# Low parts of split weights and rotary products moved from GpSimd to VectorE, and two buffers of the last layer moved to tiles that are no longer read

## The chip, the cores and the metric

The kernel runs on one core of a Trainium2 chip. The metric is the device time of one execution in microseconds (us), lower is better. The core has a matrix engine (TensorE, PE in the rows; its weight loads are PEld), VectorE (DVE), ScalarE (ACT), GpSimd (POOL) and a queue that issues transfers from device memory (SyncE, SP). Each engine takes its instructions in a fixed order; semaphores tie the engines together.

## The reference, cut to what matters

Two layers over 256 latent tokens and 256 context tokens, model width 1024. Each layer is a half-step SwiGLU, a token mixing, and a second half-step SwiGLU. In the last layer, the context tokens only give keys and values to the mixing, and the last SwiGLU runs for latent tokens alone.

```
f0/f1:  x = x + 0.5 * gate * rmsnorm((silu(y @ wg) * (y @ wu)) @ wd)      # y = modulated rmsnorm(x), wg/wu 1024 x 2816
mixing: uv, q, k, v = split(y @ w_in)
        q, k = rope(q), rope(k)              # x * cos + rotated(x) * sin, latent tokens only
        o = [gMLP gating, differential attention, windowed attention] @ w_out
        x = x + gate * rmsnorm(o)
```

## The kernel before

**Split products.** A matrix product in full precision is made of three cheaper ones. A weight tile is loaded as fp32 into a staging buffer (`stg`, three of them), ScalarE rounds it to `hi` (L233), and the low part `lo = full - hi` is a subtraction (`split_lo`, L101). TensorE then adds hi x hi, hi x lo and lo x hi. `split` (L215) cuts a tile in two or four pieces along its depth; each piece is one ScalarE instruction and one subtraction. The `hi` and `lo` buffers are three each (`wsp`), handed out in rotation; a fourth tile waits until TensorE has read the first for the last time. `wchunk` is a load followed by a split.

**Who subtracts.** With `share=True` the first piece of a tile goes to GpSimd, the others to VectorE. Shared are the weights of the token mixing (`cols`, `wv`, and `chunk` of the first layer's output projection) and the first gate and up tiles of every SwiGLU but the very first (`two` in `ffn`). The rotary embedding (`rope_evac`) is a copy by ScalarE (L690), then a shuffle (L692), a product with the sine (L693), a product with the cosine on GpSimd (L694) and a sum (L695), the other three on VectorE.

**The order.** The program is written in the order of TensorE's work; tasks (softmax chains, turns of the normalised rows) are put in at due times counted in TensorE columns, and the framework orders each engine's queue by readiness and priority. The residual chains and `first=True` splits have high priority.

**The end of the last mixing and the last SwiGLU.** `rest_tokens` (L1010) computes the last gMLP parts and the output projection for the two latent token blocks: `wr` holds two weight tiles (columns 0 to 511), `wc` two more (columns 512 to 1023, the second of them in the place of Yh and Yl that the context tokens had). The norm gate's two rows (`gate_rows`, L416) are loaded into `CU[:, 7]` and `VGf[:, 3584:4096]`, parts of tiles that the mixing uses for queries, keys and values, and are read when the projection is scaled (L1071). The tile `CU` has the tag `Ul`, `QK` the tag `Uh`: the last SwiGLU's `Uh` and `Ul` lie in the same memory and can be written when the mixing's last instruction on `QK` and on `CU` is done. The last SwiGLU begins with two groups for each token block: the first gate and up tile, then the second gate and up tile (256 columns each). The first gate, the first up and the second up tile take `wsp` buffers, behind `wr` and `wc[0]` in the rotation; the second gate tile is split into the upper halves of `Uh` and `Ul`.

Of the kernel before, what the change touches and what calls it, by code (L numbers as in the profile page):

```python
# [15 lines left out]
ALU = mybir.AluOpType  # L16
# [9 lines left out]
KB = D // P  # L26
# [37 lines left out]
def trunk(ctx: ExitStack, tc: tile.TileContext, x, c, cx, c_ctx, w_mod, b_mod, norm_pre, norm_post,  # L64
# [32 lines left out]
    def f32(ap):  # L97
        return ap.bitcast(F32)

    def split_lo(lo, full, hi, eng=nc.vector):  # L100
        eng.tensor_tensor(lo, full, f32(hi), op=ALU.subtract)  # L101


    evq, clk, busy = [], [0.0], [False]
# [107 lines left out]
                return split(v, *args[1:], **kw)  # L212
        return split(stage(*args), *args[1:], **kw)

    def split(v, nk, ncol, pair=False, into=None, share=False, pool=False):  # L215
        if into is not None:
            hi, lo = into
        else:
            hi = wsp.tile([P, 2048], F32R, tag="hi", name=nm("hi"))[:, 0:nk * ncol].rearrange(
                "p (k c) -> p k c", k=nk)  # L220
            lo = wsp.tile([P, 2048], F32R, tag="lo", name=nm("lo"))[:, 0:nk * ncol].rearrange(
                "p (k c) -> p k c", k=nk)
        if pair:
            v4 = v.rearrange("p k (v g d) -> p k v g d", v=2, g=2)
            for g in range(2):
                hv = hi[:, :, g * P:(g + 1) * P].rearrange("p k (v d) -> p k v d", v=2)
                lv = lo[:, :, g * P:(g + 1) * P].rearrange("p k (v d) -> p k v d", v=2)
                nc.scalar.activation(hv, v4[:, :, :, g, :], AF.Copy)
                split_lo(lv, v4[:, :, :, g, :], hv)
            return hi, lo  # L230
        cut = [0, nk // 4, nk // 2, nk // 2 + nk // 4, nk] if nk >= 8 else [0, nk // 2, nk]
        for a, b in zip(cut, cut[1:]):
            nc.scalar.activation(hi[:, a:b, :], v[:, a:b, :], AF.Copy)  # L233
            split_lo(lo[:, a:b, :], v[:, a:b, :], hi[:, a:b, :],
                     nc.gpsimd if pool or (share and a == 0) else nc.vector)
        return hi, lo

    def acc3(o, terms):
# [294 lines left out]
                task(("y", s), turn_y(ys, nxt, st, s[0], *((pb, T_LATE, 1.2) if s == order[-1] else (pa,))))  # L533


    def gate_up(l, e, cs, into=None, share=False):
        return (wchunk([(0, 256, w_gate[l, e, :, cs:cs + 256])], KB, 256, into=into, share=share),
                wchunk([(0, 256, w_up[l, e, :, cs:cs + 256])], KB, 256, share=share))

    def gate_up_one(l, e, cs):  # L540
        return wchunk([(0, P, w_gate[l, e, :, cs:cs + P]), (P, 256, w_up[l, e, :, cs:cs + P])], KB, 256)
# [1 line left out]
    def ffn(l, e, streams, nxt, first=None, out_order=None):  # L543
# [36 lines left out]
        for pi, (f0, nf) in enumerate(PHASES):  # L580
            Uh = big.tile([P, KB, NT], F32R, tag="Uh", name=nm("Uh"))
            Ul = big.tile([P, KB, NT], F32R, tag="Ul", name=nm("Ul"))
            for fp in range(0, nf, 2):
                cs = (f0 + fp) * P
                two = pi == 0 and fp == 0 and not first
                if pi == 0 and fp == 2 and not first:
                    continue
                rows = nxt is None
                if first and pi == 0 and fp == 0:
                    for i in range(3):  # L590
                        hidden(first[i], first[3 + i], i, full)
                    step()
                    continue
                if first and pi == 0 and fp == 2:
                    gu = [pa(), pa()]
                    w = gate_up_one(l, e, cs + P)
                    for i in range(2):
                        acc3(gu[i], yterms(w, i * P, full))
                    hidden(gu[0], gu[1], 3, full)
                    step()  # L600
                    continue
                wg, wu = gate_up(l, e, cs, share=two)
                if two:
                    into = [t[:, 4:8, :].rearrange("p a (b c) -> p (a b) c", b=2)
                            for t in (Uh, Ul)]
                    second = gate_up(l, e, cs + 256, into, True)
                    for s in range(2) if rows else streams:
                        drain(("y", s))
                        for f, (g_, u_) in ((0, (wg, wu)), (2, second)):
                            if rows:  # L610
                                gu = pa()
                                acc3_multi([(gu[:, c0:c0 + 256], rterms(w, s), c0 == 0)
                                            for w, c0 in ((g_, 0), (u_, 256))])
                                task("u", hidden_rows(gu, f, s))
                                continue
                            gus = [pa(), pa()]
                            groups = []
                            for w, c0 in ((g_, 0), (u_, 256)):
                                for i in range(2):
                                    groups.append((gus[i][:, c0:c0 + 256], yterms(w, i * P, s),  # L620
                                                   c0 == 0))
                            acc3_multi(groups)
                            for i in range(2):
                                hidden(gus[i][:, 0:256], gus[i][:, 256:512], f + i, s)
                else:
                    for i in range(2):
                        g = pa()
                        acc3(g[:, 0:n], yterms(wg, i * P, ys))
                        u = pa()
                        acc3(u[:, 0:n], yterms(wu, i * P, ys))  # L630
                        hidden(g[:, 0:n], u[:, 0:n], fp + i, full)
                step()

            drain("u")
            down(l, e, pi, f0, nf, Z, Uh, Ul, out_order or streams, nxt)
# [40 lines left out]
    def mixing(l, streams, qstreams, nxt):  # L676
# [12 lines left out]
        def rope_evac(dst, ps, scale):  # L689
            nc.scalar.activation(dst, ps, AF.Copy, scale=scale)  # L690
            sh = wk.tile([P, 256], F32, tag="t256", name=nm("shf"))
            nc.vector.stream_shuffle(sh, dst, shmask)  # L692
            nc.vector.tensor_tensor(sh, sh, ropet[:, 1, :], op=ALU.mult)  # L693
            nc.gpsimd.tensor_tensor(dst, dst, ropet[:, 0, :], op=ALU.mult)  # L694
            nc.vector.tensor_tensor(dst, dst, sh, op=ALU.add)  # L695

        def fm(w, f0, s):
# [10 lines left out]
                nc.scalar.activation(dst[:, SEQ:NT], ps[:, o:o + CTX], AF.Copy, scale=scale)  # L708

        def cols(c0, n, into=None):  # L710
            return wchunk([(0, n, W[:, c0:c0 + n])], KB, n, into=into, share=True, first=True)

        tmpw = big.tile([P, 2, KB, 256], F32R, tag="Ul", name=nm("tmpw"))
        wkq = []
# [21 lines left out]
        def rows_of(k0, n, c0, w):  # L736
            return W[k0 * P:(k0 + n) * P, c0:c0 + w]

        wv = [wchunk([(0, 512, rows_of(k0, n, VB0, 512)), (512, 640, rows_of(k0, n, VC0, P))], n, 640,
                     share=True, first=True)  # L740
              for k0, n in ((0, 3), (3, 3), (6, 2))]

        def tok_terms(ws, tb, c0, c1):
# [276 lines left out]
        def rest_tokens():  # L1020
# [19 lines left out]
            wu = cols(U0, 256)  # L1040
            for m in (("m", l, 1), ("m",) + nxt[:2]):
                drain(m)
            gp = gate_rows(l, 1, 0, [CU[:, 7, :], VGf[:, 3584:4096]])
            gate_values(wg, (0, 1))
            wr = [out_rows(kk) for kk in range(2)]
            gates(wu, XS)
# [67 lines left out]
            return (QK[:, 4 + 2 * i:6 + 2 * i, SEQ:NT] if i < 2 else CU[:, 2 * i - 3:2 * i - 1, SEQ:NT])  # L1114

        def chunk(hf, i):
            return wchunk([(0, 512, w_out[l, i * 512:(i + 1) * 512, hf * 512:(hf + 1) * 512])], 4, 512,
                          share=True)

        def oterms(ws, tb):  # L1120
            return [(Yh[:, k, ycols(tb)], Yl[:, k, ycols(tb)], ws[k // 4][0][:, k % 4, :],
# [195 lines left out]
```

## Time and profile before

| | |
|---|---|
| time, median of 3 runs | 1740.14 us (1739.44 to 1740.27) |
| the profiled execution: its time | 1744.91 us |
| its span, first to last instruction | 1743.1 us |
| TensorE busy in it | 1708.0 us (98%) |
| VectorE busy | 1257.9 us (72%) |
| GpSimd busy | 156.0 us (9%) |
| granted TensorE clock, mean | 0.995 |

The busy time of an engine is the union of its instructions' spans; a wait stands as idle time of the engine that waits, with the instruction that ended it. The granted clock is 1.00 at 2.4 GHz and 0.50 at 1.2 GHz. A row of several instructions begins with the start of the first.

### The profile page before, as it was taken

The numbers are of one execution on the slowest core, as the hardware profiler recorded it, in microseconds if no ns is written. First come the engines' busy times: TensorE is split into PE (matmuls) and PEld (weight loads), VectorE is DVE, ScalarE is ACT, GpSimd is POOL, SyncE is SP. The second block draws the span as 40 slices with busy tenths as digits, with TensorE's granted clock in tenths as the row PEclk, the third lists the DMA queues.
The fourth block names the chain that finished last, engine by engine and source line by source line (L and its number), as shares of the span: only waits on it lengthen the run. The fifth ranks groups of instructions, "written<-read, shape, count | busy, mean of one in ns | idle before, by whom it ended". The sixth has DMA issues, their size and how long they took to land.

```text
span 1743.1 us, 24539 instructions
## 1 busy us (share of the span) xinstructions
PE 1708.0 (98%) x9551; PEld 1448.2 (83%) x9551; DVE 1257.9 (72%) x2272; ACT 689.8 (40%) x1460; POOL 156.0 (9%) x161
## 2 busy tenths in 40 slices
PE   7999999999999999999999999999999999999998
PEld 4788888889977789888888898888888897789997
DVE  5889969965578577799694578799674747765555
ACT  4333213244376562332223442322232626655443
POOL 0000000022222120000000210000000322010000
PEclk9999999999999999999999999999999999999999
DMA  9666546523131143565453235655444223226552
GB/s 336 192 197 201 189 137 193 196 78 109 59 124 42 45 128 128 182 195 192 145 187 128 73 122 169 193 192 194 140 152 145 73 86 121 73 92 200 194 193 85
DMA packets 193264, 256.13 MB, mean 147 GB/s; under 512 B 7466, under 2 KB 128508, under 8 KB 193148
## 3 DMA queue, kind: packets, MB, share of 16 engines
q1 hardware_dynamic: 192380, 254.51, 44.9%
q8 instruction: 75, 1.23, 0.3%
q14 instruction: 41, 0.34, 0.1%
q0 software_dynamic: 768, 0.05, 0.0%
HBM read 253.44 MB, written 1.10 MB: 146 GB/s over the span
## 4 chain that ended last, share of the span: by engine, by line
PE 86%; DVE 7%; ACT 3%; issue 2%; POOL 1%; DMA 1%; POOLq 0%; DVEq 0%; ACTq 0%; SPq 0%
PE pa L243 27%; PE pa L247 13%; PE pb L262 6%; PE pb L256 6%; PE pb L264 6%; PE pa L256 5%; PE pa L264 5%; PE pa L262 5%; PE pb L243 3%; DVE lo L101 2%; PE pb L247 2%; PE pa L1242 1%; PE pa L785 1%; PE pc L806 1%; PE pc L883 1%
## 5 line engine op out<-in xcount | busy, mean ns | idle before, releaser
L101 DVE TENSOR_TENSOR lo<-stg,hi 128x512 fp32r<-128x512 f32 (+3 forms) x476 | 369.1, 808 | 154.4 <-ACT hi L233 127.7
L233 ACT ACTIVATE hi<-stg 128x512 fp32r<-128x512 f32 (+3 forms) x496 | 318.4, 702 | 356.1 <-PE pa L243 119.9
L243 PE MATMUL pa<-Yl,hi 128*128 128x512 f32 (+1 forms) x1168 | 415.5, 365 | 0.0
L243 PE MATMUL pa<-Yh,hi 128*128 128x512 f32 (+1 forms) x1168 | 413.2, 363 | 0.0
L349 DVE SCALAR_TENSOR_TENSOR acc<-stg,sT,acc 128x512 f32<-128x512 f32 x448 | 308.4, 746 | 9.3 <-DMA stg<-in_w_mod_dram 9.3
L247 PE MATMUL pa<-Yh,lo 128*128 128x512 f32 (+1 forms) x1168 | 258.7, 363 | 0.0
L243 PEld LDWEIGHTS pa<-Yl,hi 128*128 128x128 f32 x1168 | 220.5, 189 | 34.5
L243 PEld LDWEIGHTS pa<-Yh,hi 128*128 128x128 f32 x1168 | 220.5, 189 | 33.7
L247 PEld LDWEIGHTS pa<-Yh,lo 128*128 128x128 f32 x1168 | 202.0, 189 | 34.4 <-DVE lo L101 0.2
L256 PE MATMUL pb<-hi,Ul 128*128 128x512 f32 x400 | 156.9, 392 | 0.0
L264 PE MATMUL pb<-lo,Uh 128*128 128x512 f32 x400 | 155.8, 390 | 0.0
L262 PE MATMUL pb<-hi,Uh 128*128 128x512 f32 x400 | 155.6, 390 | 0.1
L558 ACT ACTIVATE Uh<-ha 128x512 fp32r<-128x512 f32 (+1 forms) x92 | 50.7, 551 | 220.6 <-DVE ha L556 220.6
L554 ACT ACTIVATE ht<-pa 128x512 f32<-128x512 f32 (+1 forms) x91 | 46.4, 510 | 131.9 <-PE pa L247 109.2
L262 PE MATMUL pa<-Yh,hi 128*128 128x256 f32 x368 | 91.9, 285 | 0.0
L264 PE MATMUL pa<-Yl,hi 128*128 128x256 f32 x368 | 91.3, 283 | 0.0
L556 DVE TENSOR_TENSOR ha<-ha,pa 128x512 f32<-128x512 f32 (+1 forms) x91 | 53.2, 584 | 49.0 <-PE pa L247 48.2
L262 PEld LDWEIGHTS pb<-hi,Uh 128*128 128x128 f32 x400 | 75.1, 188 | 16.0 <-DVE Z L491 0.5
L264 PEld LDWEIGHTS pb<-lo,Uh 128*128 128x128 f32 x400 | 75.1, 188 | 15.5
L256 PEld LDWEIGHTS pb<-hi,Ul 128*128 128x128 f32 x400 | 75.1, 188 | 15.4
L264 PEld LDWEIGHTS pa<-Yl,hi 128*128 128x128 f32 x368 | 70.6, 192 | 0.1
L262 PEld LDWEIGHTS pa<-Yh,hi 128*128 128x128 f32 x368 | 70.5, 192 | 0.1
(300 smaller groups left out, 2700.3 us busy)
## 6 DMA issues: line engine op xcount, KB each, us to landing
stg<-in_w_mod_dram SPq DMA_DIRECT2D x64, 1024.0 KB, 5.1
stg<-in_ffn_w_gate_dram SPq DMA_DIRECT2D x42, 1024.0 KB, 5.3
stg<-in_ffn_w_up_dram SPq DMA_DIRECT2D x42, 1024.0 KB, 5.4
stg<-in_ffn_w_down_dram SPq DMA_DIRECT2D x32, 1024.0 KB, 5.1
stg<-in_w_in_dram SPq DMA_DIRECT2D x14, 1024.0 KB, 5.0
stg<-in_ffn_w_down_dram SPq DMA_DIRECT2D x16, 768.0 KB, 4.4
mst<-in_w_mod_dram SPq DMA_DIRECT2D x16, 512.0 KB, 8.9
stg<-in_w_out_dram SPq DMA_DIRECT2D x8, 1024.0 KB, 6.8
```

Of the source, the lines that this page charges most:

```text
L101: eng.tensor_tensor(lo, full, f32(hi), op=ALU.subtract)
L233: nc.scalar.activation(hi[:, a:b, :], v[:, a:b, :], AF.Copy)
L243: nc.tensor.matmul(o, lhsT=ah, rhs=r, start=(i == 0), stop=(i == n - 1))
L247: nc.tensor.matmul(o, lhsT=al, rhs=bh, start=(i == 0), stop=(i == n - 1))
L256: nc.tensor.matmul(o, lhsT=al, rhs=bh, start=False, stop=last, skip_group_check=True)
L262: nc.tensor.matmul(o, lhsT=ah, rhs=bh, start=(first and k == 0), stop=False, skip_group_check=True)
L264: nc.tensor.matmul(o, lhsT=ah, rhs=bl, start=False, stop=False, skip_group_check=True)
L349: nc.vector.scalar_tensor_tensor(a, v[:, k, :], sc, a, op0=ALU.mult, op1=ALU.add)
L554: nc.scalar.activation(t, g, AF.Tanh, scale=0.5)
L556: nc.vector.tensor_tensor(a, a, u, op=ALU.mult)
L558: nc.scalar.activation(uh, a, AF.Copy)
L785: nc.tensor.matmul(sc[:, 0:n], lhsT=QK[64 * m:64 * m + 64, 4 + h, tb * P:(tb + 1) * P], rhs=QK[64 * m:64 * m + 64, h, k0:k1], start=True, ...
```

## The change

The argument that sent a piece to GpSimd is gone: every low part is a VectorE subtraction. The rotary product with the cosine is on VectorE too. In the last layer, the norm gate's rows go to `S[:, 2]`, the residual stream's rows of a context token block, which nothing reads after the first SwiGLU of that layer. In the last SwiGLU, the first gate tile takes the upper halves of `Uh` and `Ul` and the second gate tile takes a `wsp` buffer; in the other SwiGLUs the second gate tile stays in `Uh` and `Ul`.

```diff
-    def split_lo(lo, full, hi, eng=nc.vector):
-        eng.tensor_tensor(lo, full, f32(hi), op=ALU.subtract)
+    def split_lo(lo, full, hi):
+        nc.vector.tensor_tensor(lo, full, f32(hi), op=ALU.subtract)
...
             nc.scalar.activation(hi[:, a:b, :], v[:, a:b, :], AF.Copy)
-            split_lo(lo[:, a:b, :], v[:, a:b, :], hi[:, a:b, :],
-                     nc.gpsimd if pool or (share and a == 0) else nc.vector)
+            split_lo(lo[:, a:b, :], v[:, a:b, :], hi[:, a:b, :])
...
-                wg, wu = gate_up(l, e, cs, share=two)
+                into = [t[:, 4:8, :].rearrange("p a (b c) -> p (a b) c", b=2) for t in (Uh, Ul)]
+                wg, wu = gate_up(l, e, cs, into if two and rows else None)
                 if two:
-                    into = [t[:, 4:8, :].rearrange("p a (b c) -> p (a b) c", b=2)
-                            for t in (Uh, Ul)]
-                    second = gate_up(l, e, cs + 256, into, True)
+                    second = gate_up(l, e, cs + 256, None if rows else into)
...
-            nc.gpsimd.tensor_tensor(dst, dst, ropet[:, 0, :], op=ALU.mult)
+            nc.vector.tensor_tensor(dst, dst, ropet[:, 0, :], op=ALU.mult)
...
-            gp = gate_rows(l, 1, 0, [CU[:, 7, :], VGf[:, 3584:4096]])
+            gp = gate_rows(l, 1, 0, [S[:, 2, 0:512], S[:, 2, 512:1024]])
```

The other lines of the diff take `share=True` out of `gate_up`, `cols`, `wv` and `chunk`. `rows` is true in the last SwiGLU alone.

## Rows read from the trace of the kernel before

**Rows 1.** The page: the span, and the busy time of TensorE with its share.

```profile
span 1743.1 us, 24539 instructions
...
PE 1708.0 (98%) x9551; PEld 1448.2 (83%) x9551; DVE 1257.9 (72%) x2272; ACT 689.8 (40%) x1460; POOL 156.0 (9%) x161
```

**Rows 2.** The busy time by stretch, of all engines. Columns: the stretch, its length, then busy us and instructions of each engine, the mean granted clock, the DMA engines' busy share and their GB/s. The stretches are the start, the attention part of the first layer's mixing and of the second's, the first groups of the last SwiGLU, and the end.

```profile
0.00:30.00 30.00, 18.64 (x126) 11.90 (x127) 13.61 (x46) 13.48 (x25) 3.92 (x14) 1.00 1.00 333
...
480.00:600.00 120.00, 113.73 (x744) 89.37 (x742) 83.25 (x225) 80.12 (x240) 22.17 (x17) 0.97 0.20 67
...
1440.00:1540.00 100.00, 96.06 (x611) 75.66 (x610) 72.82 (x168) 70.80 (x188) 15.97 (x14) 0.98 0.25 85
1540.00:1560.00 20.00, 16.62 (x121) 15.79 (x119) 13.63 (x24) 8.15 (x21) 4.07 (x4) 0.91 0.61 197
...
1710.00:1743.10 33.10, 25.77 (x130) 21.66 (x128) 15.12 (x21) 9.50 (x16) 4.32 (x4) 0.95 0.13 48
```

**Rows 3.** Who TensorE waited for, in three stretches, one after the other: 480 to 660 us, 1380 to 1540 us, 1540 to 1560 us. Columns: waiting instruction, what ended the wait, us in total, times, longest us.

```profile
PE pa L769 <- DVE p L796: 2.9, 4, 1.5
...
PE pb L243 <- POOL lo L101: 0.5, 1, 0.5
...
PE pa L264 <- DVE lo L101: 2.0, 2, 1.5
PE pa L262 <- ACT hi L233: 0.7, 1, 0.7
PE pa L264 <- POOL lo L101: 0.6, 1, 0.6
```

**Rows 4.** GpSimd's subtractions (L101) and its rotary products (L694), in the views of these two lines: count, duration in ns (min/median/max), first and last start, and shapes.

```profile
L101 POOL TENSOR_TENSOR lo<-stg,hi x32: 730/1734/2896, 382.7 to 1546.9; 128x512 fp32r<-128x512 f32 x19, 128x640 fp32r<-128x640 f32 x6, 128x1024 fp32r<-128x1024 f32 x5, 128x256 fp32r<-128x256 f32 x2
L101 POOL TENSOR_TENSOR Ul<-stg,Uh x3: 1297/1540/1667, 640.7 to 1540.3; 128x512 fp32r<-128x512 f32 x3
L101 POOL TENSOR_TENSOR tmpw<-stg,tmpw x2: 1440/1445/1450, 400.7 to 1383.1; 128x512 fp32r<-128x512 f32 x2
...
L694 POOL TENSOR_TENSOR QK<-QK,ropet x16: 735/916/924, 436.7 to 1408.7; 128x256 f32<-128x256 f32 x16
L694 POOL TENSOR_TENSOR CU<-CU,ropet x6: 726/970/1160, 497.1 to 1469.7; 128x256 f32<-128x256 f32 x6
```

**Rows 5.** Groups of VectorE's instructions by line and shape: first of 1050 to 1370 us, where GpSimd does next to nothing, then of the whole run. Columns: line, engine, operation, out<-in, shapes, count, busy us, mean ns of one, idle us before them and what ended it.

```profile
L101 DVE TENSOR_TENSOR lo<-stg,hi 128x512 fp32r<-128x512 f32 x74 | 48.1, 687 | 21.9 <-ACT hi L233 18.4 <-PE pa L247 3.4
L101 DVE TENSOR_TENSOR lo<-stg,hi 128x1024 fp32r<-128x1024 f32 x18 | 21.8, 1217 | 4.3 <-PE pa L247 3.4 <-ACT hi L233 0.9
...
L101 DVE TENSOR_TENSOR Yl<-fy,Yh 128x256 fp32r<-128x256 f32 x16 | 5.9, 420 | 0.0
L693 DVE TENSOR_TENSOR shf<-shf,ropet 128x256 f32<-128x256 f32 x22 | 18.6, 870 | 0.1
L695 DVE TENSOR_TENSOR QK<-QK,shf 128x256 f32<-128x256 f32 x16 | 10.0, 652 | 0.1
L695 DVE TENSOR_TENSOR CU<-CU,shf 128x256 f32<-128x256 f32 x6 | 2.6, 426 | 1.3 <-POOL CU L694 0.8
```

**Rows 6.** The timeline of GpSimd, VectorE and TensorE at three places of the first layer's mixing and one of the second's. Columns: start us, duration us, engine, line, operation, out<-in, shapes, count, and in brackets the idle time before it with what ended it.

```profile
550.64 2.41 POOL L101 TENSOR_TENSOR lo<-stg,hi 128x1024 fp32r<-128x1024 f32 x1 [1.46 <-ACT hi L233]
...
551.46 1.60 DVE L794 SCALAR_TENSOR_TENSOR rs<-rs,nlam,ss 128x1 f32<-128x1 f32 x1
...
553.91 0.66 PE L769 MATMUL pa<-ident,p 128*128 128x128 f32 x4 [0.61 <-DVE p L796]
...
561.01 1.48 DVE L794 SCALAR_TENSOR_TENSOR rs<-rs,nlam,ss 128x1 f32<-128x1 f32 x1
...
563.34 0.66 PE L769 MATMUL pa<-ident,p 128*128 128x128 f32 x4 [1.51 <-DVE p L796]
...
567.79 0.22 DVE L794 SCALAR_TENSOR_TENSOR rs<-rs,nlam,ss 128x1 f32<-128x1 f32 x1
...
1415.04 0.83 DVE L101 TENSOR_TENSOR lo<-stg,hi 128x640 fp32r<-128x640 f32 x1 [1.64 <-ACT hi L233]
```

**Rows 7.** From the last output projection to the last SwiGLU: the load of the second up tile (SP), the split of the second gate tile into Uh (ACT, a row of its line's view) and Ul (POOL), the last instructions that read CU (a turn on PE, a row of the tile's view; two products of L1071 on DVE), and TensorE's last reads of `wc` with its waits.

```profile
L233 ACT ACTIVATE Uh<-stg x4: 627/630/633, 1509.3 to 1512.8; 128x512 fp32r<-128x512 f32 x4
...
L834 PE MATMUL pa<-ident,CU x4: 271/272/273, 1521.9 to 1522.2; 128*128 128x128 f32 x4
L1071 DVE TENSOR_TENSOR zg<-pb,CU x2: 678/682/685, 1511.8 to 1539.5; 128x512 f32<-128x512 f32 x2
...
1538.64 1.12 PE L256 MATMUL pb<-hi,Yl 128*128 128x256 f32 x8
...
1540.27 1.67 POOL L101 TENSOR_TENSOR Ul<-stg,Uh 128x512 fp32r<-128x512 f32 x1 [1.23 <-DVE zg L1071]
1540.94 0.37 SPq L205 DMA_DIRECT2D stg<-in_ffn_w_up_dram  x1
...
1546.16 0.63 ACT L233 ACTIVATE hi<-stg 128x512 fp32r<-128x512 f32 x1 [4.72 <-DMA stg<-in_ffn_w_up_dram]
1551.95 0.47 PE L264 MATMUL pa<-lo,Yh 128*128 128x256 f32 x1 [1.50 <-DVE lo L101]
```

**Rows 8.** VectorE before and at the boundary, as in rows 2.

```profile
1522.00:1534.00 12.00, 11.41 (x82) 10.05 (x81) 5.64 (x15) 9.37 (x29) 1.11 (x2) 1.00 0.01 2
1534.00:1546.00 12.00, 11.49 (x89) 10.98 (x88) 11.82 (x16) 5.92 (x14) 4.87 (x4) 1.00 0.32 102
```

More of the change, by code (lines that the diff above doesn't have):

```diff
@@ L213, in wchunk, with split @@
         return split(stage(*args), *args[1:], **kw)
-    def split(v, nk, ncol, pair=False, into=None, share=False, pool=False):
+    def split(v, nk, ncol, pair=False, into=None):
         if into is not None:
@@ L533, in down, with gate_up @@
                 task(("y", s), turn_y(ys, nxt, st, s[0], *((pb, T_LATE, 1.2) if s == order[-1] else (pa,))))
-    def gate_up(l, e, cs, into=None, share=False):
-        return (wchunk([(0, 256, w_gate[l, e, :, cs:cs + 256])], KB, 256, into=into, share=share),
-                wchunk([(0, 256, w_up[l, e, :, cs:cs + 256])], KB, 256, share=share))
+    def gate_up(l, e, cs, into=None):
+        return (wchunk([(0, 256, w_gate[l, e, :, cs:cs + 256])], KB, 256, into=into),
+                wchunk([(0, 256, w_up[l, e, :, cs:cs + 256])], KB, 256))
     def gate_up_one(l, e, cs):
@@ L710, in cols @@
         def cols(c0, n, into=None):
-            return wchunk([(0, n, W[:, c0:c0 + n])], KB, n, into=into, share=True, first=True)
+            return wchunk([(0, n, W[:, c0:c0 + n])], KB, n, into=into, first=True)
         tmpw = big.tile([P, 2, KB, 256], F32R, tag="Ul", name=nm("tmpw"))
@@ L739, in mixing @@
         wv = [wchunk([(0, 512, rows_of(k0, n, VB0, 512)), (512, 640, rows_of(k0, n, VC0, P))], n, 640,
-                     share=True, first=True)
+                     first=True)
               for k0, n in ((0, 3), (3, 3), (6, 2))]
@@ L1116, in chunk @@
         def chunk(hf, i):
-            return wchunk([(0, 512, w_out[l, i * 512:(i + 1) * 512, hf * 512:(hf + 1) * 512])], 4, 512,
-                          share=True)
+            return wchunk([(0, 512, w_out[l, i * 512:(i + 1) * 512, hf * 512:(hf + 1) * 512])], 4, 512)
         def oterms(ws, tb):
```

## The prediction

> **What bounds the kernel now.** First the page: TensorE is busy 1708.0 of 1743.1 us [rows 1], so the matrix work sets the time, the number of matrix instructions does not change, and only the 35.1 us in which TensorE stands, and what a halved clock costs it, can be won. Then the busy time by stretch, to see where those 35 us lie: 11.4 in the first 30 us and 7.3 after 1710 us, where the change touches nothing (the first tiles were never shared, and the last residual has no split ahead of it); 6.3 between 480 and 600 us, 3.9 between 1440 and 1540 us, and 3.4 in the 20 us at the start of the last SwiGLU [rows 2]. These last three, 13.6 us, are the field. The long SwiGLU stretches between them have no gap, and a faster or slower VectorE is worth nothing there.
>
> Next, who ended the waits. In the mixing it is mostly the softmax chain (L769 waits for VectorE's L796, 2.9 us in four waits); near 1417 us it is GpSimd's low part, 0.5 us; in the last SwiGLU it is the split alone: 2.0 us for VectorE's low parts, 0.7 for ScalarE's high part, 0.6 for GpSimd's [rows 3]. Last the timeline at two of the softmax waits. L794 works on one column and takes 0.22 us undisturbed, but 1.60 and 1.48 us where it starts while GpSimd is inside a low part; the first ends at 553.06, when GpSimd ends (550.64 + 2.41 = 553.05). The wait that the view puts down to VectorE is a wait for GpSimd [rows 6].
>
> **What is moved, and its price.** GpSimd made 32 + 3 + 2 = 37 low parts and 16 + 6 = 22 rotary products [rows 4]. On VectorE a low part of 512 columns costs 0.687, of 1024 columns 1.217, of 256 columns 0.420 [rows 5], of 640 columns 0.83 [rows 6]. That is 24 x 0.687 + 5 x 1.217 + 2 x 0.42 + 6 x 0.83 = 28.4 us; a rotary product costs what the undisturbed sum of the same size does, 0.426 [rows 5], so 22 x 0.426 = 9.4 us. VectorE gets 37.8 us more to do.
>
> Against it stands what VectorE lost to GpSimd. The sine products beside the cosine products took 0.870 instead of 0.426: 22 x 0.444 = 9.8 us; the sums behind them in QK 0.652 instead of 0.426: 16 x 0.226 = 3.6 us [rows 5]; the two L794 1.38 and 1.26 us [rows 6]. These alone give 16.0 of the 37.8 back, without the blocked low parts, which no single row sums up. One piece at a time: a 512-column piece holds GpSimd for 1.4 to 1.7 us and costs VectorE 0.687; a rotary product holds it for 0.92 and costs 0.426 [rows 4, 5]. So where the two engines collide VectorE comes out ahead, and where they don't it is busy 69% in the first mixing (83.25 of 120 us) and 73% in the second [rows 2], so there is room. I take zero for VectorE's extra work on the path, with bounds: a gain of the blocked waits, below, and a loss of half the work moved into the stretches with waits (rival B).
>
> The rule behind the blocking is in the Trainium skill, SBUF — State Buffer, section "Who interferes with whom": a GpSimd instruction that reads SBUF and a VectorE instruction with two SBUF inputs share a read port, and the later one waits for the whole of the earlier one. The trace agrees for L693 (0.870 beside 0.92 us of GpSimd), and L794, whose inputs are one column, is held just as long. By the rule alone, every overlap would come back to VectorE, and the sum below would be at its better end.
>
> **The sum, by places.**
> 1. *Last SwiGLU's first groups, 3.4 us of standing.* Why it stands: the second up tile is loaded only at 1540.94, because the staging buffers are full; ScalarE waits 4.72 us for it, until 1546.16, and TensorE waits until 1551.95 for its low parts [rows 7]. The buffers are full because the first gate tile waits for `wr`'s buffers, and the second gate tile, whose high part was ready at 1509.3 to 1512.8, for `CU`: GpSimd's piece of `Ul` starts at 1540.27, behind L1071's product with the gate row in `CU` (1539.5) [rows 7]. Afterwards the first gate tile needs `QK` and `CU` alone. The last read of `CU` is then the turn at 1522.2 [rows 7]. VectorE is idle 6.4 us between 1522 and 1534 and needs 4 x 0.687 = 2.7 us for the four low parts [rows 5, 8], which come out of the busy stretch 1534 to 1546 (11.82 of 12 us [rows 8]). The staging buffer comes free near 1526 instead of 1540.9; the second up tile lands 5.2 us after its issue (1540.94 to 1546.16, its landing and ScalarE's start [rows 7]), near 1531. It then has to wait for the third `wsp` buffer, which `wc[0]` leaves when its eight products of 1538.64 are done, at 1539.8: high pieces to 1542, low pieces from about 1543. TensorE, which reached the low part of 1551.95 after 3.3 us of waits [rows 3, 7], would ask for it at 1548.6; it would be there near 1545. I take 3.0 of 3.4 us. Bounds 0 to 3.4.
> 2. *The clock there.* It is 0.91 over 20 us [rows 2]: (1 - 0.91) x 20 x 2 = 3.6 us at 1.2 GHz, which cost up to 1.8 us, right behind the waits. I take 1.5, bounds 0 to 1.8.
> 3. *GpSimd's low part at 1417 us*: 0.5 us [rows 3]. VectorE does a 640-column piece in 0.83 us [rows 6] where GpSimd's median piece takes 1.73 [rows 4], so the low part comes 0.9 us sooner; two on VectorE, one behind the other, take 1.66, still less than one on GpSimd. I take 0.5.
> 4. *The two blocked softmax chains*: waits of 0.61 and 1.51 us [rows 6]. VectorE must do the 1.217 us low part itself, in part in idle time before the chain, so L794 comes 0.8 us sooner rather than 1.4. I take 0.6 + 0.9 = 1.5; bounds 0 to 2.1.
> 5. *The gate rows in `S[:, 2]`*: two transfers on SP as before, whose target is free sooner; the product L1071 reads another address at the same cost. Nothing, but for what it does in 1. Bounds are the same as in 1.
> 6. *The rotation afterwards*: the second gate tile now holds a buffer to the end of the first four groups, so the next up tile's split starts one group later. TensorE needs it one accumulation later still. I take 0; one late piece would cost 0.6 (a ScalarE piece, 0.63 [rows 7]).
>
> Sum 3.0 + 1.5 + 0.5 + 1.5 = 6.5. The profiled execution took 1744.91 us; the sum makes it 1738.4. The median of the runs is 4.8 us below the profiled execution; with the same sum it comes to **1733.6 us**.
>
> **Rivals.**
> *A. The tiles give nothing.* The second up tile still comes late, since `wc[0]`'s buffer and VectorE's queue (residual first) hold it in place of the staging buffer. For it: 1534 to 1546 is full on VectorE [rows 8]; against it, 2.7 us leave that stretch. Then terms 1 and 2 go: 1740.1 - 2.0 = 1738.1.
> *B. VectorE becomes what TensorE waits for.* The moved pieces stand in one queue with the softmax chain; while L794 waits behind them, so do L796 and TensorE. GpSimd has 22.2 + 16.0 of its 156.0 busy us between 480 and 600 and between 1440 and 1540 us [rows 1, 2], a quarter; a quarter of 37.8 is 9.3 us. If all of that comes on the path and nothing of the blocking comes back, it stands against the 3.5 us of terms 1 and 3, with the clock lost again: 1740.1 + 9.3 - 3.5 = 1745.9, slower. It decides from 3.5 us on the path, four tenths of what is moved there. For it: those waits are softmax waits [rows 3]. Against: the undisturbed prices are below GpSimd's.
> The Trainium skill, Perfetto Trace Analysis, section "Optimizing Scalar/DVE Operations", speaks for B: with VectorE saturated, handing work to GpSimd may make sense, though it adds that the shared port may make it useless. VectorE is at 69 to 73% here, which is not saturated.
> *C. More comes.* With the chains shorter, the half clock in both mixings goes too: (1 - 0.97) x 120 x 2 = 7.2 and (1 - 0.98) x 100 x 2 = 4.0 us at 1.2 GHz [rows 2], up to 5.6 us of time: 1728.0.
>
> **How the numbers follow.** Forecast 0.57, A 0.17, B 0.11, C 0.15. The forecast's own range is 1730 to 1737. A measurement tells 0.2%, 3.5 us, from no change. Faster by over 3.5 us (below 1736.7): C, nearly all of the forecast and the better third of A, 0.73. Slower (above 1743.6): two thirds of B, 0.07. Same: the rest, 0.20. The range leaves out the better half of C and the worse half of B: 1727 to 1741.
>
> **What would show it.** No GpSimd row of L101 or L694; L693 near 0.42 us, no L794 over 0.3 but behind `pow`; the first gate tile's low parts in Ul between 1522 and 1534; the second up tile issued before 1535; no wait at L264 and a clock of 1.00 in the last SwiGLU's first groups. Wrong it would be if L769 waited longer for L796 than 2.9 us, if L264 still waited over 1 us, or if the queues came out in another order and new waits stood elsewhere.

## The result, and the profile after

The changed kernel takes 1731.98 us (median of 5 runs, 1730.28 to 1733.87) against 1740.14 before (1739.44 to 1744.4): a ratio of 0.9947, 95% interval 0.9935 to 0.996. The forecast was 1733.6 in a range of 1727 to 1741, and faster. The same kernel once more, beside other runs of before, gave 0.9935 (0.9922 to 0.9948).

In the traces the gain is larger. The span goes from 1743.1 [rows 1] to 1730.2 us, because the profiled execution of before lay 4.8 us above that median. In the three later comparisons the median of before was 1742 to 1743 (1742.34 against 1731.66 beside the second run of the changed kernel), so the usual gap is 10 to 12 us. First the page of the changed kernel, the lines that answer to [rows 1].

```profile
span 1730.2 us, 24450 instructions
...
PE 1703.2 (98%) x9551; PEld 1447.4 (84%) x9551; DVE 1248.0 (72%) x2331; ACT 690.1 (40%) x1460; POOL 80.1 (5%) x102
```

TensorE stands 27.0 us where it stood 35.1. VectorE, which got 37.8 us more to do, is busy 9.9 us *less* (1257.9 before), and GpSimd 75.9 us less. Next the busy time by stretch, as [rows 2], with two stretches more: the entries of two SwiGLUs.

```profile
480.00:600.00 120.00, 115.34 (x767) 91.17 (x767) 84.23 (x239) 82.95 (x245) 8.21 (x8) 0.99 0.20 67
640.00:662.00 22.00, 22.00 (x187) 22.00 (x186) 17.45 (x35) 7.05 (x16) 0.00 (x0) 1.00 0.51 167
1010.00:1042.00 32.00, 31.76 (x267) 31.56 (x266) 25.61 (x51) 12.43 (x29) 0.87 (x1) 1.00 0.37 117
1440.00:1540.00 100.00, 96.93 (x629) 78.33 (x628) 76.94 (x189) 69.89 (x189) 7.87 (x8) 0.97 0.35 116
1540.00:1560.00 20.00, 20.00 (x169) 19.98 (x169) 10.69 (x23) 9.46 (x23) 0.00 (x0) 1.00 0.23 80
```

The same two added stretches in the kernel before:

```profile
640.00:662.00 22.00, 21.38 (x181) 21.18 (x180) 18.21 (x34) 10.00 (x24) 3.94 (x4) 1.00 0.51 168
1010.00:1042.00 32.00, 30.66 (x256) 30.23 (x255) 23.38 (x47) 13.95 (x34) 4.56 (x5) 1.00 0.32 105
```

Length minus the first busy number is TensorE's standing. It falls from 6.3 to 4.7 us in the first mixing, from 3.9 to 3.1 in the second, from 3.4 to nothing in the last SwiGLU [rows 2], and by 0.6 and 1.1 us at the two entries. With 0.6 between 1380 and 1440 us (59.23 busy us before, 59.83 after) that is 8.2 us, all of the 8.1 that TensorE stands less.

Then VectorE's groups between 380 and 1560 us, first of the changed kernel: the rotation (L693 to L695), the one-column product L794, and three lines that the prediction did not look at, the residual sum (L426), its copy into the matmul type (L458) and the norm's scaling (L434).

```profile
L426 DVE SCALAR_TENSOR_TENSOR S<-Z,r,S 128x512 f32<-128x512 f32 x24 | 17.1, 749 | 4.7 <-POOL r L411 4.4
L458 DVE CAST Yh<-yf 128x512 fp32r<-128x512 f32 x36 | 15.0, 421 | 10.1 <-ACT yf L453 10.0
...
L434 DVE TENSOR_SCALAR Z<-S,r 128x512 f32<-128x512 f32 x25 | 11.3, 484 | 7.6 <-POOL r L411 7.6
...
L693 DVE TENSOR_TENSOR shf<-shf,ropet 128x256 f32<-128x256 f32 x22 | 9.2, 417 | 0.0
...
L694 DVE TENSOR_TENSOR QK<-QK,ropet 128x256 f32<-128x256 f32 x16 | 6.7, 418 | 0.0
...
L695 DVE TENSOR_TENSOR QK<-QK,shf 128x256 f32<-128x256 f32 x16 | 6.7, 417 | 0.1
...
L794 DVE SCALAR_TENSOR_TENSOR rs<-rs,nlam,ss 128x1 f32<-128x1 f32 x24 | 5.2, 218 | 0.6
```

The last three and L794 in the kernel before, where their lines are L427, L459 and L435:

```profile
L459 DVE CAST Yh<-yf 128x512 fp32r<-128x512 f32 x36 | 22.0, 617 | 13.4 <-ACT yf L454 13.3
...
L427 DVE SCALAR_TENSOR_TENSOR S<-Z,r,S 128x512 f32<-128x512 f32 x24 | 20.2, 881 | 4.7 <-POOL r L412 4.5
...
L435 DVE TENSOR_SCALAR Z<-S,r 128x512 f32<-128x512 f32 x24 | 12.7, 563 | 7.6 <-POOL r L412 7.6
...
L794 DVE SCALAR_TENSOR_TENSOR rs<-rs,nlam,ss 128x1 f32<-128x1 f32 x24 | 7.9, 329 | 0.7
```

L693 is at 0.417 us (0.870 in [rows 5]) and L794 at 0.218 instead of 0.329. But the copies lost more than L794 did: 22.0 us for 36 of them before, 15.0 now. Together with L427 (3.1 us) and L435 (1.9, for equal counts), the three lines give back 12 us that the prediction did not count.

Where the time went can also be read by pairing the same ScalarE and VectorE instructions in both traces and taking the difference of their starts (worked out from the two traces; each row is a median over 20 us):

| us of before | place | changed minus before, us |
|---|---|---|
| 460 | start of the first attention part | 0.0 |
| 540 | inside it | -1.2 |
| 580 | its end | -4.3 |
| 700 to 960 | after the entry of the next SwiGLU | -5.4 |
| 1060 to 1340 | after the entry of layer two's SwiGLU | -6.8 |
| 1440 | second attention part begins | -8.1 |
| 1520 | end of the second mixing | -7.0 |
| 1580 to the end | last SwiGLU, first groups done | -12.9 |

The granted clock has a part in three of these steps (rows in the last experiment below): the changed kernel has 3.4 us less at 1.2 GHz between 540 and 600 us and again between 1520 and 1580, and 3.4 us more between 1440 and 1520, each worth up to 1.7 us.

### The profile page after: what moved, and what is told of

The parts are those of the page before. It is cut to its first block, busy times and chain, and to the rows that moved or that the text cites. A ratio compares the mean times of both kernels' runs of the same rounds, so it can differ in the third digit from the quotient of the medians.

```text
span 1730.2 us, 24450 instructions
## 1 busy us (share of the span) xinstructions
PE 1703.2 (98%) x9551; PEld 1447.4 (84%) x9551; DVE 1248.0 (72%) x2331; ACT 690.1 (40%) x1460; POOL 80.1 (5%) x102
## 4 chain that ended last, share of the span: by engine, by line
PE 92%; DVE 4%; ACT 2%; POOL 1%; issue 1%; DMA 0%; POOLq 0%; DVEq 0%; ACTq 0%
PE pa L242 27%; PE pa L246 14%; PE pa L255 6%; PE pa L261 6%; PE pa L263 6%; PE pb L255 6%; PE pb L261 6%; PE pb L263 6%; PE pb L242 4%; PE pb L246 2%; PE pa L1242 1%; PE pa L785 1%; PE pc L883 1%; DVE lo L101 1%; PE pc L806 1%
## 5 line engine op out<-in xcount | busy, mean ns | idle before, releaser
L101 DVE TENSOR_TENSOR lo<-stg,hi 128x512 fp32r<-128x512 f32 (+4 forms) x508 | 386.4, 797 | 159.9 <-ACT hi L233 114.5
```

What stands on the lines that cost most here:

```text
L101: nc.vector.tensor_tensor(lo, full, f32(hi), op=ALU.subtract)
```

## Experiments

Two theories stood after the result. **P**: VectorE and GpSimd hold each other up at the memory they share, and the change wins what VectorE lost there. **L**: GpSimd's low parts came too late for TensorE, because it takes two to three times as long for a piece. Beside them the split between the edits was open: the prediction gave 4.5 of its 6.5 us to the tiles.

**Engines alone.** The two tile edits undone.

```diff
-                wg, wu = gate_up(l, e, cs, into if two and rows else None)
+                wg, wu = gate_up(l, e, cs)
-                    second = gate_up(l, e, cs + 256, None if rows else into)
+                    second = gate_up(l, e, cs + 256, into)
...
-            gp = gate_rows(l, 1, 0, [S[:, 2, 0:512], S[:, 2, 512:1024]])
+            gp = gate_rows(l, 1, 0, [CU[:, 7, :], VGf[:, 3584:4096]])
```

> Only the engine moves: every low part and every cosine product on VectorE; the gate rows stay in CU and VG, and the second gate tile of the last SwiGLU stays in Uh and Ul. If the blocking between GpSimd and VectorE is what the mixing paid for, about 7 us come off up to the end of the last mixing, as in the trace of the changed kernel (its residual at 1526 us comes 6.9 us earlier), and the first groups of the last SwiGLU still stand for about 3 us, because the second up tile is still loaded near its old place: 1733 to 1736. If the moved work fills VectorE's queue and the gain was the tiles', the time is 1739 or more.

Measured: 1733.4 us, ratio 0.9943 (0.9931 to 0.9956). TensorE's waits between 1534 and 1562 us:

```profile
PE pa L263 <- DVE lo L101: 0.7, 2, 0.4
```

Of 3.4 us of waits 0.7 are left, though no tile has moved; the 3 us of standing that were expected did not come. The second up tile is issued at 1534.07 instead of 1540.94 [rows 7]. Of these 6.9 us, 5.2 are the lead that the whole kernel has at 1500 us (paired starts, as in the table); against its own TensorE the tile comes 1.7 us sooner.

**Tiles alone.** The kernel before with the tile edits; low parts and cosine products shared as before.

```diff
-                wg, wu = gate_up(l, e, cs, share=two)
+                wg, wu = gate_up(l, e, cs, into if two and rows else None, share=two)
...
-                    second = gate_up(l, e, cs + 256, into, True)
+                    second = gate_up(l, e, cs + 256, None if rows else into, True)
...
-            gp = gate_rows(l, 1, 0, [CU[:, 7, :], VGf[:, 3584:4096]])
+            gp = gate_rows(l, 1, 0, [S[:, 2, 0:512], S[:, 2, 512:1024]])
```

> Only the two tile edits: gate rows in S, first gate tile in Uh and Ul; GpSimd keeps its low parts and cosine products. If the standing in the last SwiGLU came from the full staging buffers, the second up tile is issued before 1530, the 3.4 us of standing and the 1.8 us of half clock between 1540 and 1560 go, and nothing changes before 1500: 1735 to 1737. If it was GpSimd's blocking of the residual and of the low parts there, the standing stays above 2 us: 1738 or more.

Measured: 1739.77 us, ratio 0.9977 (0.9967 to 0.9987); the median of before beside it was 1743.38. TensorE's waits between 1534 and 1562 us:

```profile
PE pc L573 <- DVE ha L569: 0.2, 1, 0.2
```

Nothing moves by more than 0.2 us ahead of 1500 us; the waits in the last SwiGLU fall to 0.2 us, and from 1580 us on it is 4.8 us ahead of before. So each half of the change removes most of that standing by itself: between 1500 and 1580 us 4.7 us are won by the engines, 4.6 by the tiles, 5.9 by both (the low clock's stretch there included). By the times the tiles are worth some 4 us alone (ratio 0.9977) and 1 to 2 on top of the engines (1733.4 against 1731.98 and 1731.66), which the intervals do not separate from nothing.

**The gate rows back in `CU` and `VG`.**

```diff
-            gp = gate_rows(l, 1, 0, [S[:, 2, 0:512], S[:, 2, 512:1024]])
+            gp = gate_rows(l, 1, 0, [CU[:, 7, :], VGf[:, 3584:4096]])
```

> The changed kernel with the gate rows back in CU and VG. If what matters is when CU is read for the last time, the first gate tile's low parts now start behind the last product with the gate row, near 1532 on this kernel's clock, when TensorE is about to ask for them, and the staging buffers are full again: the last SwiGLU's first groups stand 3 us or more, 1735 to 1739. If the rows' place does not matter, 1731 to 1733.

**The old order of the gate tiles.** The second gate tile in `Uh` and `Ul` also in the last SwiGLU, gate rows in `S[:, 2]`.

```diff
-                wg, wu = gate_up(l, e, cs, into if two and rows else None)
+                wg, wu = gate_up(l, e, cs)
-                    second = gate_up(l, e, cs + 256, None if rows else into)
+                    second = gate_up(l, e, cs + 256, into)
```

> The changed kernel with the second gate tile back in Uh and Ul and the first in the rotating buffers; the gate rows stay in S. If the gain needs only one staging buffer to come free early, this does as well: the second gate tile is split as soon as CU is dead, the second up tile is loaded before 1530, 1731 to 1733. If it needs the first gate tile split early, because VectorE's queue is full between 1527 and 1539, TensorE waits for the first groups' low parts: 1734 or more.

Measured: 1732.57 us, ratio 0.9939 (0.9924 to 0.9954), for the first, and 1732.13, 0.9934 (0.9921 to 0.9947), for the second; neither can be told from the changed kernel by its time. In the traces the loads of the second up tile can: 1522.19 in the changed kernel, 1523.09 with the old order, 1533.87 with the rows in `CU`. The last has one wait that the others don't have:

```profile
PE pa L261 <- ACT hi L233: 1.6, 1, 1.6
```

So it is the gate rows' place, not the swap of the gate tiles, that lets the tile be loaded early; the time is hardly touched by it.

**The cosine product back on GpSimd**, all low parts on VectorE.

```diff
-            nc.vector.tensor_tensor(dst, dst, ropet[:, 0, :], op=ALU.mult)
+            nc.gpsimd.tensor_tensor(dst, dst, ropet[:, 0, :], op=ALU.mult)
```

> The changed kernel with one edit undone: the rotary product with the cosine (L694) is on GpSimd again, all low parts stay on VectorE. Theory P (what VectorE loses to GpSimd through the memory they share is what the change wins): L693 is near 0.87 and the sums in QK near 0.65 us again, 22 x 0.44 + 16 x 0.23 = 13 us more for VectorE, against 9.4 us of products less. The mixings lose 0 to 2 us: 1732 to 1734. Theory L (GpSimd's slowness in handing over the low parts is what cost): the same VectorE rows, but no time, 1732. Both together say that rotation is the smaller part of the change.

Measured: 1732.73 us, ratio 0.9946 (0.9932 to 0.9959). VectorE's rotation rows:

```profile
L693 DVE TENSOR_TENSOR shf<-shf,ropet 128x256 f32<-128x256 f32 x22 | 17.8, 833 | 0.0
...
L695 DVE TENSOR_TENSOR QK<-QK,shf 128x256 f32<-128x256 f32 x16 | 6.1, 411 | 0.0
```

L693 is at 0.833 us again, 8.6 us of blocking in all (the sums stay at 0.411, against the expectation). By the medians it costs about 1 us (1731.98 and 1731.66 for the changed kernel), which the intervals do not separate from nothing; in the trace TensorE stands 28.4 us instead of 27.0. So hardly anybody waits for VectorE there.

**The low parts' first pieces back on GpSimd**, the cosine on VectorE, the tile edits in.

```diff
-            split_lo(lo[:, a:b, :], v[:, a:b, :], hi[:, a:b, :])
+            split_lo(lo[:, a:b, :], v[:, a:b, :], hi[:, a:b, :],
+                     nc.gpsimd if pool or (share and a == 0) else nc.vector)
```

> The changed kernel with the other engine edit undone: the first piece of each formerly shared low part is on GpSimd again, the cosine product stays on VectorE, the tile edits stay. If the low parts carry the gain, as both theories P and L have it, it is within 2 us of the kernel with tile edits alone (0.9977 of the time before, 3 to 4 us faster than before, so 1736 to 1738 where before is at 1740), with L794 at 1.4 to 1.6 us in two or more places again. If the rotary product carries it, 1732 to 1734.

Measured: 1739.74 us, ratio 0.9988 (0.9979 to 0.9998): the time of the tiles alone. As far as the times tell, the low parts carry all of the engine edit. What TensorE waited for at the first attention part (two lines) and at the entry of layer two's SwiGLU (two lines):

```profile
PE pa L768 <- DVE p L795: 3.0, 4, 1.5
PE pc L805 <- ACT pT L770: 1.7, 2, 1.0
...
PE pb L449 <- ACT yf L454: 0.7, 1, 0.7
PE pb L449 <- DVE Z L435: 0.6, 1, 0.6
```

They are those of the kernel before: 2.9 [rows 3] and 1.7 us there in the first stretch, and the same 0.7 and 0.6 at the entry. In the changed kernel they are 2.4, 1.0, 0.2 and none.

**Idle squares on GpSimd.** The changed kernel, and beside each formerly shared first piece GpSimd squares the high part into a scratch that nobody reads. This leaves no work out and adds no result, so nobody waits for a square. What GpSimd makes in the changed kernel too, norm factors (L411) and gate products (L508), can still stand behind the squares.

```diff
             split_lo(lo[:, a:b, :], v[:, a:b, :], hi[:, a:b, :])
+            if pool or (share and a == 0):
+                for k in range(a, b):
+                    for c in range(0, ncol, 320):
+                        m = min(320, ncol - c)
+                        h = f32(hi[:, k, c:c + m])
+                        nc.gpsimd.tensor_tensor(shadow[:, 0:m], h, h, op=ALU.mult)
```

> The changed kernel, every low part and product on VectorE, plus idle work on GpSimd: at each formerly shared first piece GpSimd squares the high part into a scratch that nobody reads (320 columns at a time, so a 512-column piece gives two). Nobody waits for a result, so GpSimd's slowness can't cost anything; only what it does to others can. Theory P: VectorE's two-input instructions beside these squares stretch to the length of the squares, L794 is over 1 us again in several places, and the time goes up by 3 to 6 us against the changed kernel, 1735 to 1738. Theory L: the time stays within 1 us of the changed kernel's, 1731 to 1733, whatever VectorE's rows show.

Measured: 1748.84 us, ratio 1.004 (1.0026 to 1.0054): 17 us slower than the changed kernel, far more than either theory had. GpSimd's largest group and what TensorE waited for in three stretches (480 to 600, 640 to 662, 1010 to 1042 us):

```profile
L242 POOL TENSOR_TENSOR shadow<-hi 128x256 bf16<-128x256 f32 (+2 forms) x74 | 67.0, 905 | 202.1 <-ACT hi L235 198.7
```

```profile
PE pa L775 <- DVE p L802: 5.6, 4, 2.9
...
PE pb L456 <- ACT yf L461: 1.9, 1, 1.9
...
PE pb L456 <- ACT yf L461: 1.3, 1, 1.3
PE pb L456 <- DVE Z L442: 1.1, 1, 1.1
```

With 6.9 us on `Uh`, `Ul` and `tmpw` pieces GpSimd is in the squares for 73.9 us, in the places where the real low parts of the run before this one took it 63.6. L falls as the main cause: here GpSimd makes no low part that could be late (and in the kernel before TensorE's waits for one came to 1.1 us in all [rows 3]), and the softmax waits are 5.6 us instead of 2.4, the entries 1.9, 1.3 and 1.1 instead of 0.2 in all. L794 (L800 here) reached 0.56 us, not the 1 us that P had expected; the blocking lies in the long pieces, the copies and the norm.

One of GpSimd's other results does come late. At the first of these entries a norm factor (L419, from `v`, ready at 642.75) stands behind squares for 0.6 us:

```profile
641.68 1.75 POOL L242 TENSOR_TENSOR shadow<-hi 128x256 bf16<-128x256 f32 x2 [2.27 <-ACT hi L235]
643.38 0.55 POOL L419 TENSOR_TENSOR r<-v,negh 128x1 f32<-128x1 f32 x1
...
643.97 0.88 DVE L442 TENSOR_SCALAR Z<-S,r 128x512 f32<-128x512 f32 x2 [1.22 <-POOL r L419]
```

So up to 0.6 of the 1.9 us there is lateness after all. It is the only one of the 38 factors of this line; in the kernel before none stands behind a low part (worked out from the traces).

A part of the 17 us is the clock: the mean granted clock of the six executions is 0.992 to 0.995, where the changed kernel has 0.996 to 0.999, and the trace has 20.5 us at 1.2 GHz between 480 and 1560 us, where the changed kernel has 10.2. Why it falls more often here no run shows.

The kernel with the real low parts on GpSimd loses 8 us to the changed kernel. So being held up costs more than the 28.4 us of work that GpSimd takes off VectorE are worth. Of the 9 us between the two runs half is the clock: at 0.995 three executions of each are on record, 1742.3 to 1742.5 and 1747.1 to 1747.6 us, 4.7 us apart by their medians. That the squares hold VectorE up for longer is not the other half: by the count under the next run VectorE lost about 34 us to the real low parts and 31.7 to the squares. The 28.4 us of relief are what is left to name; no run measured them by themselves.

**Idle copies in place of the squares**: one input instead of two.

```diff
-                        nc.gpsimd.tensor_tensor(shadow[:, 0:m], h, h, op=ALU.mult)
+                        nc.gpsimd.tensor_copy(shadow[:, 0:m], h)
```

> As the kernel with idle squares on GpSimd, but GpSimd copies the high part (one input) where it squared it (two inputs). If any reading of GpSimd holds up VectorE's two-input instructions, they stretch to the length of the copies, and with copies of about half to all the length of the squares the time is 1738 to 1749 us. If it takes two inputs on GpSimd, VectorE's rows are as in the changed kernel and the time is within 2 us of it.

Measured: 1734.41 us, ratio 0.9957 (0.9942 to 0.9971), 2 to 3 us slower than the changed kernel and below the 1738 to 1749 us that were expected if copies hold VectorE up. GpSimd's group:

```profile
L242 POOL CAST shadow<-hi 128x256 bf16<-128x256 f32 (+2 forms) x74 | 46.8, 632 | 207.5 <-ACT hi L235 204.7
```

Summing over VectorE's instructions that overlap GpSimd, each against the median of its form elsewhere (worked out from the traces), VectorE lost 4.3 us in the changed kernel, 15.9 with the copies and 31.7 with the squares. So copies hold it up too, 0.22 us for each us of theirs against 0.37 for the squares (11.6 of 51.6 and 27.4 of 73.9, with those on `Uh`, `Ul` and `tmpw`), and by the medians at a sixth of the time. But the clock differs here too: four of the five executions with copies ran at 0.998 or 0.999, those with squares at 0.992 to 0.995. At one clock the copies cost about 4 us and the squares about 15 (an estimate, worked out at the end of this section), so the price is much nearer to the proportion of VectorE's losses, 11.6 to 27.4 us, than the medians have it. That a short hold-up hides behind other work and a long one reaches past it would fit what is left, but no run measured it by itself.

**Smaller pieces.** The changed kernel, the output projection's tiles split into four pieces of 512 columns.

```diff
-        cut = [0, nk // 4, nk // 2, nk // 2 + nk // 4, nk] if nk >= 8 else [0, nk // 2, nk]
+        cut = [0, nk // 4, nk // 2, nk // 2 + nk // 4, nk] if nk >= 8 or fine else [0, nk // 2, nk]
```

> The changed kernel with the output projection's weight tiles split in four pieces of 512 columns instead of two of 1024. In the changed kernel the wait of 1.85 us at 561 us (L769 for L796) stands because a low part of 1024 columns, 1.22 us, starts on VectorE 0.1 us before L794 could. If VectorE's own queue is what is left of that wait, a piece of 0.69 us shortens it by about 0.5 us, and the time is 1731 to 1732, too little to tell by the times alone. If something else sets it (ScalarE's high part of 1.05 us ahead of the exponential's sum), it stays at 1.8 us.

Measured: 1733.1 us, ratio 0.9946 (0.9932 to 0.996). The longest wait of the changed kernel, on VectorE and TensorE (columns as in [rows 6]):

```profile
558.94 0.17 DVE L793 RECIPROCAL rs<-ss 128x2 f32<-128x2 f32 x1 [1.25 <-ACT p L790]
559.02 1.22 DVE L101 TENSOR_TENSOR lo<-stg,hi 128x1024 fp32r<-128x1024 f32 x1
...
560.16 0.21 DVE L794 SCALAR_TENSOR_TENSOR rs<-rs,nlam,ss 128x1 f32<-128x1 f32 x1
...
560.50 0.75 DVE L796 SCALAR_TENSOR_TENSOR p<-p,rs,p 128x512 f32<-128x512 f32 x1
...
561.30 0.66 PE L769 MATMUL pa<-ident,p 128*128 128x128 f32 x4 [1.86 <-DVE p L796]
```

and the same place with smaller pieces:

```profile
559.58 0.17 DVE L793 RECIPROCAL rs<-ss 128x2 f32<-128x2 f32 x1 [1.35 <-ACT p L790]
559.66 0.69 DVE L101 TENSOR_TENSOR lo<-stg,hi 128x512 fp32r<-128x512 f32 x1
...
560.27 0.21 DVE L794 SCALAR_TENSOR_TENSOR rs<-rs,nlam,ss 128x1 f32<-128x1 f32 x1
...
560.40 0.69 DVE L101 TENSOR_TENSOR lo<-stg,hi 128x512 fp32r<-128x512 f32 x1
...
561.00 0.74 DVE L796 SCALAR_TENSOR_TENSOR p<-p,rs,p 128x512 f32<-128x512 f32 x1
...
561.80 0.66 PE L769 MATMUL pa<-ident,p 128*128 128x128 f32 x4 [2.60 <-DVE p L796]
```

The wait gets longer, 2.60 us. One piece stands between L793 and L794 and now a second one between L794 and L796: the order on VectorE puts a piece into each gap of the chain, and two of 0.69 us are more than one of 1.22. The wait is VectorE's own queue, as the expectation had it; its remedy was wrong. An order with the chain's three instructions in a row was not measured.

**The kernels before and after again**, for second profiles.

> The kernel before, unaltered, for a second profile. Its first profiled execution took 1744.91 us, 4.8 above its median, and its runs lie between 1739 and 1747. If that spread is one of where the half-clock stretches fall, the second profile has the same instructions at the same times up to such a stretch and differs by steps of about 1.7 us from there on; if transfers that come late make it, other waits of TensorE appear.

> The changed kernel, unaltered, beside the three others on one chip and for a second profile. Its ratio should come out at 0.9947 again within 0.0015. If the half-clock stretch at 1473 us that lasted 6.83 us in its first profile is its own, it is there again; if it is chance, it stands elsewhere or lasts 3.41 us, and the profile's span differs by about 1.7 us for each 3.41 us.

Measured: before 1742.21 us against 1742.1 (ratio 1.0001, 0.9992 to 1.0011); after 1731.66. In the second profile of each the instructions start where they did in the first, within 0.2 us to the end for after, and within 0.1 us up to 1520 us for before, which then gains 0.8 us in the last SwiGLU (waits of 2.8 us there instead of 3.4). The stretches at the low clock stand in the same places, to within 0.7 us. Those between 480 and 1560 us in the first profile of before (the granted clock is the third number from the end):

```profile
575.20:582.00 6.80, 6.80 (x22) 4.69 (x23) 3.58 (x12) 4.16 (x12) 1.01 (x1) 0.55 0.01 1
1483.80:1487.20 3.40, 3.40 (x18) 3.40 (x18) 2.50 (x8) 0.31 (x1) 1.61 (x1) 0.51 0.33 83
1552.00:1555.40 3.40, 3.40 (x16) 3.40 (x17) 1.85 (x4) 0.00 (x0) 0.00 (x0) 0.52 0.29 56
```

and in the first of the changed kernel, whose last row is the place where before has its third:

```profile
562.00:565.40 3.40, 3.40 (x8) 1.61 (x9) 2.34 (x4) 1.34 (x5) 0.00 (x0) 0.51 0.26 77
1473.50:1480.30 6.80, 6.80 (x34) 6.80 (x33) 5.58 (x12) 2.27 (x6) 1.91 (x1) 0.50 0.48 155
1552.00:1555.40 3.40, 3.40 (x32) 3.40 (x30) 2.63 (x6) 2.46 (x5) 0.00 (x0) 1.00 0.00 0
```

In the second profiles the same windows show 0.50, 0.59 and 0.58, and 0.51 and 0.52. That is about 13.6 us near 1.2 GHz before and 10.2 after, so between these profiles the clock's part in the gain is up to 1.7 us.

The executions that were not profiled say that this is not fixed by the kernel. Each has its mean granted clock on record: for the kernel before, 60 executions lie between 0.994 (1747.08 us) and 0.999 (1739.01 to 1741.25 us, fourteen of them), and their time grows by about 1.1 us for each 0.001 that the clock is lower. Their mean clock is 0.9970, that of ten executions of the changed kernel 0.9967, so over all executions the clock has no part in the gain. At 0.996 before took 1742.3 to 1744.7 us in ten executions and the changed kernel 1731.4 to 1733.9 in six.

Brought to a clock of 0.997 with that 1.1 us, the means are, as an estimate: before 1742.5, low parts back on GpSimd 1740.2, tiles alone 1739.5, engines alone 1733.2, the changed kernel 1731.4, idle copies 1735.4, idle squares 1746.1. The gain is then 11 us, and the engine edit carries most of it.

## Why the prediction was right, and where it was not

The sign holds and the time, 1731.98 against 1733.6, lies near. That it lies so near is in part luck: the sum was too small (6.5 us, against 12.9 between the profiles and about 11 at one clock), and the base made up for it, since the median shown, 1740.14, lay below what before usually takes. Nor could the sum be carried over to that base whole. The profiled execution of before ran at 0.995, and the executions of before under 1740.5 us whose clock is on record ran at 0.998 or 0.999, so the low clock that term 2 wins back was hardly in them.

1. *Last SwiGLU, 3.0 us.* All 3.4 us went. The prediction's cause was half of it: it gave the gain to the tiles alone. The run without them has 0.7 us of waits left, and the run with them alone 0.2, so either half is enough. What the step missed is that the engine edit also advances the second up tile, to 1534.07 (1.7 us against its own TensorE), and has GpSimd's share of the low parts there, for which TensorE waited 0.6 us [rows 3], made on VectorE. Rival A, that the tiles give nothing, falls as a statement on the tiles alone (4 us) and comes near for the tiles on top of the engines.
2. *The clock, 1.5.* Right between the two profiles: 3.4 us at the low clock are gone there. Over all executions the mean clock is the same before and after, so over all of them the term won nothing. Rival C did not come: in the profiles the first mixing has 3.4 us less of it, the second 3.4 more.
3. *GpSimd's low part at 1417 us, 0.5.* Right: that wait is gone.
4. *The softmax chains, 1.5.* The size is right (the standing there fell from 6.3 to 4.7 us), the place is not, so the size is luck. The first wait of 0.61 went. The second, 1.51 in [rows 6], became 1.86: L794 takes 0.21 us now, but stands behind VectorE's own 1.22 us low part. That is rival B's mechanism, in this one place. What went instead is 0.7 us at L806 (1.7 to 1.0) and small waits.
5. *Gate rows in `S`, nothing but for what they do in 1.* With the engines moved, but the rows in `CU`, the second up tile is issued near 1534; the rows' new place brings it to 1522, with either order of the gate tiles. (The first gate tile's low parts in `Ul` start from 1516.0 to 1521.4; the kernel is 7.0 us ahead there, so this is the 1522 to 1534 of the forecast.)
6. *The rotation afterwards, 0.* Right: no wait of TensorE shows between 1540 and 1700 us.

The term that was missing is VectorE's blocked copies, residual sums and scalings at the entries of the SwiGLUs and of the second mixing. One instance in the kernel before, with TensorE's wait behind it:

```profile
645.58 1.29 POOL L101 TENSOR_TENSOR lo<-stg,hi 128x512 fp32r<-128x512 f32 x1
645.64 1.91 DVE L435 TENSOR_SCALAR Z<-S,r 128x512 f32<-128x512 f32 x2 [0.44 <-POOL r L412]
...
652.16 0.55 PE L449 MATMUL pb<-ident,Z 128*128 128x128 f32 x3 [0.62 <-ACT yf L454]
```

Two scalings of 0.48 us each take 1.91 where GpSimd's low part started 0.06 us ahead of them; in the changed kernel this pair takes 0.89. The prediction listed what two SBUF inputs cost (the rotary rows and L794, 16.0 us) and said that the blocked low parts were not summed up; it left out the residual sums, which have two as well, and the copies and scalings, which have one. The section of the Trainium skill that it cited, SBUF — State Buffer, "Who interferes with whom", names these: copy, cast and tensor_scalar can enter a two-port mode and can then contend with GpSimd too. The trace agrees: L459, a cast, takes 0.422 us at the median and up to 1.830 in the kernel before, at most 0.429 in the changed one. With both rules of that section the list would have had 12 us more, 3.1 by the residual sums and 8.9 by the copies and scalings. On the path it is 2.0 us of standing: TensorE's waits at L449 were 0.6, 1.3 and 0.3 us at the three entries and are 0.2 now. The run with the low parts back on GpSimd has them again, at 0.6, 1.3 and 1.5.

In the second mixing 0.9 us less standing was not forecast either. 3.1 us of the 12.9 stay without a row: 8.1 are less standing, 1.7 the clock, and the rest lies in TensorE's busy time, whose ends are modelled.

Rival B, slower by up to 5.8 us, did not come: VectorE, busy 72% of the time, took over 37.8 us and got 47.7 back.

## What to carry to other kernels

Work that GpSimd took over here was paid by VectorE as well: before sharing, list VectorE's instructions that overlap it, with one input as well as two, and compare their longest with their median. What such blocking costs in time is decided by who waits behind it: the rotation lost 8.6 us of VectorE for about 1 us of time, the copies, residual sums and scalings lost 12 us and had 2.0 us of TensorE's standing behind them. When two edits aim at one wait, ask of each alone what it leaves; here either was enough, and their gains did not add. And look at the granted clock of every execution before two times a few us apart are compared: here one kernel's executions spread over 8 us with it.

## What the hardware showed that was not expected

Idle GpSimd work, 74 us of squares that nobody reads, makes this kernel 17 us slower, some 15 of them at one clock. Two profiled executions of one program agree within 0.1 to 0.2 us over 1500 us, though over all its executions the mean clock goes from 0.994 to 0.999. And VectorE's busy time fell by 9.9 us when it got 37.8 us more work: the rows above (rotation 12.8, L794 2.7, the three lines 12.0) make up 27.5 of the 47.7 us between them, low parts on VectorE itself some 7 more (L101's pieces of 512 columns 0.710 to 0.698, of 1024 columns 1.255 to 1.218), and the rest is spread over many lines.
